# Weights loaded by piece into six tiles, later output stores, and the inverse's exchange issued by GpSimd

## The chip, the cores and the metric

The kernel runs on one core of one Trainium2 chip. The metric is the device time of one execution in microseconds, lower is better. The core has five engines that run their own instruction streams in order: TensorE (PE; weight loads are shown as PEld), VectorE (DVE), ScalarE (ACT), GpSimd (POOL) and SyncE (SP), which here only issues transfers. Transfers (DMA) run beside all of them.

## The reference

One layer of a hybrid decoder: 256 tokens, width 2048, all in float32. A gated delta rule branch (16 query and key heads, 32 value heads of 128) and an mLSTM branch (8 heads) run side by side on the same normalised input; their outputs are projected, gated, merged, projected again and added to the input.

```python
shift, scale, gate = jnp.split(jax.nn.silu(c) @ w_ada + b_ada, 3, axis=-1)
h = rms_norm(x, norm_pre_w) * (1.0 + scale[:, None]) + shift[:, None]
proj = h @ w_in
...
o_a = gated_delta_rule(q_a, k_a, v_a, g_log, beta)      # chunks of 64, a unit lower triangular solve in each
o_a = rms_norm(o_a, gdn_norm_w) * jax.nn.silu(gdn_z)
y_a = o_a @ w_proj_gdn
...
h_b = mlstm_chunkwise(q_b, k_b, v_b, ml_i + mlstm_b_i, ml_f + mlstm_b_f)
h_b = jax.nn.sigmoid(ml_o) * rms_norm(h_b, mlstm_norm_w) * jax.nn.silu(ml_z)
y_b = h_b @ w_proj_mlstm
merged = jax.nn.sigmoid(gate_a) * y_a + jax.nn.sigmoid(gate_b) * y_b
out = merged @ w_out
return x + gate[:, None] * rms_norm(out, norm_post_w)
```

The matrices hold some 375 MB, and each is read once. Products keep float32 accuracy with two parts of each operand: a high part `hi` in the narrower type float32r and the rest `lo`, so that one product is `hi*hi + hi*lo + lo*hi`, three passes of TensorE (`mm3`, L245 to L247).

## The kernel before

**The weight stream.** `Stream` (L64) holds a list of weight units in the order of the program. A unit is one load of up to 128 x 2048 float32 (1 MB) into one of three tiles `raw` (`load_w`, L161). It is used in pieces of 1024 columns: `prep_w` (L205) has ACT cast a piece into `whi` (L176) and DVE subtract to give `wlo` (L180), four buffers of each, and then `use` runs the products of the piece on TensorE (L247 for token-major results `pn`, `py`, `pw`; L658 and L662 for transposed ones `pt`). `_loads` issues the load of a unit as soon as the unit three places before it has had its last piece split, so a slot comes free after both of its halves have been split.

**Side work.** Beside the products of each piece, generators in `Side` emit the instructions of the recurrences; a `yield` puts the rest one piece (a step) later, `wait(n)` n steps. The order on every engine is thus fixed when the program is built. All transfers but a handful are issued by SP, in program order, and one that waits holds up those behind it.

**One period of the delta rule branch** (`gdn_period`, eight of them, `zg` 0 to 7; some 80 us each) loads the weights of two pairs of heads (`z` 0 and 1), and emits for each pair `gdn_stage1`: rows `gb` are fetched (L740), GpSimd masks them (`dd`, L747), ACT takes exponentials (L755 to L757), and DVE forms the matrices `au` (L816). `block_rows` (L894) then stores the 32 x 32 diagonal blocks to `ud` in DRAM (L900, four transfers for each pair). `base_inverse` (L903) inverts them: fetch `ug` from `ud` (L909, four transfers, each block broadcast four times), 32 rows of substitution on DVE over `xx` (L928 to L934), store `xx` to `xd` (L937, one transfer), and fetch it turned as `xcmp` (L941, four transfers). These 4 + 4 + 4 + 1 + 4 = 17 transfers are the exchange. From `xcmp`, ACT and DVE fill `x0`, `ycmp` and `y0` (L945 to L950), and `gdn_stage2` (L957) doubles the blocks on TensorE: `mp` (L978), its copy `pcm` (ACT, L983), `mx` (L994), `mq` and `mz` (L1012, with the copy `p` of L1018 between), then `pa` (L1039, which needs the values `rr` that ACT scales at L889), `pb`, `pc` and `po`. The normalised result goes through `oT` (L1110) to `o_dr` in DRAM (L1112); the output projections read it later (`ya`). The substitution and the stage 2 of one period run in the next one or two periods.

Four mLSTM groups follow, with the gate units between (a 1 MB unit of `w_ada` that DVE alone multiplies and adds, L1306 to L1313), then the output projections `py`, the merge and `pw`.

Of the kernel before, what the change touches and what calls it, by code (L numbers as in the profile page):

```python
# [7 lines left out]
F32 = mybir.dt.float32  # L8
F32R = mybir.dt.float32r
AF = mybir.ActivationFunctionType  # L10
ALU = mybir.AluOpType
# [4 lines left out]
P = 128  # L16
S = 256
D = 2048
KC = D // P
# [12 lines left out]
class Side:  # L32
# [4 lines left out]
    def __init__(self):  # L37
        self.gens = []
        self.t = 0
        self.debt = 0.0  # L40
# [23 lines left out]
class Stream:  # L64


    def __init__(self, load, side, ahead=3):
        self.side, self.ahead = side, ahead
        self.load = (load, "w", 3)
        self.units, self.items, self.rings = [], [], {}  # L70
        self.loaded = self.used = self.prepared = self.pending = 0

    def add(self, src, prep, use, pieces=2, after=None, on_load=None, load=None):
        load, ring, bufs = load or self.load
        r = self.rings.setdefault(ring, [])
        u = dict(src=src, prep=prep, use=use, after=after, on_load=on_load, load=load, done=False,
                 before=r[-bufs] if len(r) >= bufs else None)
        r.append(u)
        i = len(self.units)
        self.units.append(u)  # L80
        for h in range(pieces):
            self.items.append((i, h, h == pieces - 1))

    def _loads(self):

        while self.loaded < len(self.units):
            u = self.units[self.loaded]
            if u["before"] is not None and not u["before"]["done"]:
                return
            u["raw"] = u["load"](u["src"])  # L90
            if u["on_load"]:
                u["on_load"]()
            self.loaded += 1

    def run(self):
        self._loads()
        while self.used < len(self.items):
            while self.prepared < len(self.items) and self.pending <= self.ahead:
                i, h, last = self.items[self.prepared]
                u = self.units[i]  # L100
                self.pending += u["use"] is not None
                u["p", h] = u["prep"](h, u["raw"])
                u["done"] = last
                self.prepared += 1
                self._loads()
            i, h, last = self.items[self.used]
            u = self.units[i]
            self.used += 1
            if u["use"]:
                self.pending -= 1  # L110
                u["use"](h, *u["p", h])
            if last and u["after"]:
                u["after"]()
            if u["use"]:
                self.side.step()
# [3 lines left out]
def hybrid_layer_kernel(  # L119
# [25 lines left out]
    V, A, T, G, SP = nc.vector, nc.scalar, nc.tensor, nc.gpsimd, nc.sync  # L145
# [3 lines left out]
    wp = ctx.enter_context(tc.tile_pool(name="wp", bufs=2))  # L149
# [8 lines left out]
        SP.dma_start(t, src)  # L158
        return t

    def load_w(src):  # L161
        raw = wp.tile([P, 2048], F32, name="raw", tag="raw", bufs=3)
        c = 0
        for i, s_ in enumerate(src if isinstance(src, tuple) else (src,)):
            if isinstance(src, tuple) and len(s_.shape) == 3:
                SP.dma_start(raw.rearrange("p (k g c) -> p k g c", k=4, g=2)[:, :, i], s_)
                continue
            dst = raw[:, c:c + s_.shape[1] * (s_.shape[2] if len(s_.shape) == 3 else 1)]
            c += dst.shape[1]
            if len(s_.shape) == 3:  # L170
                dst = dst.rearrange("p (k n) -> p k n", k=s_.shape[1])
            SP.dma_start(dst, s_)
        return raw

    def split(src, hi, lo, eng=None):
# [10 lines left out]
    def split_w(src, hi, lo):  # L186

        n = src.shape[1]
        if early:
            eng = early.pop(0)  # L190
            A.copy(hi, src)
            for c in (slice(0, 512), slice(512, 1024)) if eng is G else (slice(0, 1024),):
                low(src[:, c], hi[:, c], lo[:, c], eng)
            if len(early) == 5:
                for k in (10, 12):
                    x_scale(k)
            return
        share[0] += share[1] * n
        if share[0] >= n:
            share[0] -= n  # L200
            split(src, hi, lo, G)
        else:
            split(src, hi, lo)

    def prep_w(h, raw, width=2048):  # L205
        n = min(1024, width - h * 1024)
        hi = wp.tile([P, 1024], F32R, name="whi", tag="whi", bufs=4)
        lo = wp.tile([P, 1024], F32R, name="wlo", tag="wlo", bufs=4)
        if begin:
            begin.pop()(raw[:, 0:n], hi, lo)  # L210
            return hi, lo
        split_w(raw[:, h * 1024:h * 1024 + n], hi[:, 0:n], lo[:, 0:n])
        return hi, lo

    freed = [-1] * 4
# [10 lines left out]
    def gfree(t):  # L226
        freed[slots[1].pop(id(t))[0]] = side.t
# [21 lines left out]
    side = Side()  # L249
    bp = x0 = y0 = None  # L250
# [3 lines left out]
    sil = cp.tile([P, KC], F32, name="sil")  # L254
# [42 lines left out]
    def ada_tile():  # L297
        return sp.tile([P, 2048], F32, name="ar", tag="ar", bufs=ADA_BUFS)

    def load_ada(src):  # L300
        raw = ada_tile()
        SP.dma_start(raw, src)
        return raw
# [114 lines left out]
    stream = Stream(load_w, side, 1)  # L418
# [315 lines left out]
    def wait(n):  # L734
        for _ in range(n):
            yield
# [157 lines left out]
    def block_rows(res, z):  # L894

        if z == 0:
            res["ud"] = dr.tile([4, 8, 32, 32], F32, name="ud", tag="ud", bufs=2)
        auv = res["au", z].rearrange("p h (b c) -> p (h b) c", b=2)
        for q in range(4):
            SP.dma_start(res["ud"][q, 4 * z:4 * z + 4].rearrange("m j i -> j m i"),  # L900
                         auv[32 * q:32 * q + 32, :, 256 + 32 * q:288 + 32 * q])

    def base_inverse(zg, res, zr):  # L903

        ud = res["ud"]
        xd = dr.tile([8, 4, 4, 8, 32], F32, name="xd", tag="xd", bufs=2)
        ug = bp.tile([P, 32, 32], F32, name="ug", tag="ug", bufs=1)
        for q in range(4):
            SP.dma_start(ug[32 * q:32 * q + 32],  # L909
                         ud[q].rearrange("m j i -> m (j i)").unsqueeze(0).broadcast_to([4, 8, 1024]))  # L910
        yield from wait(5)
        most = ROOM_US if zg else FIRST_ROOM_US
# [6 lines left out]
        xx = bp.tile([P, 8, 32], F32, name="xx", tag="xx", bufs=1)  # L919
        tmp = bp.tile([P, 8, 2, 32], F32, name="tmp", tag="tmp", bufs=1)  # L920
        V.tensor_copy(xx, eunit)
        for i in range(1, 32, 2):
            w = min(2, 32 - i)
            nq = (i + w - 2) // 4 + 1
            n = i + w
# [8 lines left out]
                V.scalar_tensor_tensor(xx[:, 0:nq, i + 1], xx[:, 0:nq, i], nsu[:, i // 2:i // 2 + 1],  # L934
                                       xx[:, 0:nq, i + 1], op0=ALU.mult, op1=ALU.add)
        yield from wait(1)
        SP.dma_start(xd.rearrange("qq q rg m i -> (q rg m) qq i"), xx)  # L937
        yield from wait(2)
        xcmp = bp.tile([P, 8, 32], F32, name="xcmp", tag="xcmp", bufs=1)
        for q in range(4):  # L940
            SP.dma_start(xcmp[32 * q:32 * q + 32], xd[:, q])  # L941
        yield from wait(3)
        side.debt += 1.1
        ycmp = bp.tile([P, 8, 32], F32, name="ycmp", tag="ycmp", bufs=1)
# [1 line left out]
        for q in range(4):  # L946
            c = slice(32 * q, 32 * q + 32)
# [9 lines left out]
    def gdn_stage2(zg, res, zr):  # L957
# [15 lines left out]
        for j in range(4):  # L973
            for i in range(2):
                m = 2 * j + i
                for t in range(2):
                    r, o = 64 * t, 64 * t + 32
                    T.matmul(pss[t][(o, r)[i]:(o, r)[i] + 32, j * 32:(j + 1) * 32], um(m)[r:r + 32, o:o + 32],  # L978
                             yc[r:r + 32, m], start=True, stop=True)
        for t in range(2):  # L980
            r, o = 64 * t, 64 * t + 32
# [7 lines left out]
        for j in range(4):  # L989
            for i in (1, 0):  # L990
                m = 2 * j + i
# [40 lines left out]
        rr = res["rr"].rearrange("p b z (h d) -> p b (z h d)", h=2)  # L1032
# [39 lines left out]
        for z in range(2):  # L1072
            junk = bp.tile([P, P], F32, name="junk", tag="sq", bufs=1)
            for blk in range(2):
                for h in range(2):
# [9 lines left out]
                               op0=ALU.mult, op1=ALU.add)  # L1085
# [18 lines left out]
        for z in range(2):  # L1104
            for h in range(2):
                for blk in range(2):
                    T.transpose(pts[z][:, h * S + blk * P:h * S + (blk + 1) * P], ons[z][:, blk, h], ident)
        for z in range(2):
            oT = bp.tile([P, 2, S], F32, name="oT", tag="oT")
            A.activation(oT.rearrange("p h t -> p (h t)"), pts[z], AF.Copy, scale=late_c["gnw"][:, 0:1])  # L1110
            gfree(pts[z])
            SP.dma_start(o_dr[4 * zg + 2 * z:4 * zg + 2 * z + 2].rearrange("h d t -> d h t"), oT)  # L1112

    def period_tail(zg, ps, qs, res, zr):
# [180 lines left out]
    gate_half = []  # L1295

    def add_gate_unit():

        gate_at[1] += KC
        if gate_at[1] < 34 or gate_at[0] == KC:  # L1300
            return
        gate_at[1] -= 34
        i = gate_at[0]
        gate_at[0] += 1

        def prep(h, raw):  # L1306
            side.debt += 2.4
            for q in range(2):
                if i == 0:
                    gate_half.append(bp.tile([P, 1024], F32, name=f"gacc{q}", tag=("ug", "rr")[q], bufs=1 + q))  # L1310
                    V.tensor_scalar(gate_half[q], raw[:, q * 1024:(q + 1) * 1024], sil[:, 0:1], None, op0=ALU.mult)
                else:
                    V.scalar_tensor_tensor(gate_half[q], raw[:, q * 1024:(q + 1) * 1024], sil[:, i:i + 1],  # L1313
                                           gate_half[q], op0=ALU.mult, op1=ALU.add)
            if i == KC - 1:
                side.add(gate_sum())
            return ()
        stream.add(w_ada[32 + i], prep, None, 1)

    def gate_sum():  # L1320
        yield
# [312 lines left out]
```

## Time and profile before

| | us |
|---|---|
| median of 3 runs (lowest to highest) | 1574.93 (1571.59 to 1575.77) |
| profiled execution, its time | 1578.37 |
| profiled execution, span from first to last instruction | 1576.6 |
| mean granted TensorE clock | 0.995 of full |
| busy: ACT, POOL | 971.1, 269.9 |
| DMA: 397.49 MB, mean | 252 GB/s |

The page's busy time counts an engine as busy from the start of an instruction to its end; a matmul's end is modelled. POOL is busy nearly only in the first 240 us. From 400 to 1000 us the eight periods show in the slices of the page: one slice of 39.4 us with DVE at 95% busy, the next with it at 80% and DMA at 85%. In the rows, "start, length, engine, line, operation, out<-in" stand in that order, and a bracket tells how long the engine stood idle before and what ended that.

### The profile page before, as it was taken

To read this page: it belongs to the slowest core of one execution; us is meant where nothing else is said; L and a number is where in the kernel's file an instruction comes from. 1 tells how busy PE (TensorE), PEld (TensorE's weight loads), DVE (VectorE), ACT (ScalarE), POOL (GpSimd) and SP (SyncE) were. 2 spreads that over 40 slices of the span, in tenths; PEclk is the share of its full clock that TensorE was granted. 3 is DMA by queue.
4 is the path that set the end of the run, shared out by engine and by line. 5 is a ranking of instruction groups with operands and counts; after the bars stand their busy time and mean duration, and the time that the engine had idled before them with its cause. 6 is when DMAs were issued, how large, how long until landed. Compare 5 with 4: busy or idle time off the path is not lost.

```text
span 1576.6 us, 22531 instructions
## 1 busy us (share of the span) xinstructions
PE 1554.4 (99%) x8256; PEld 1297.2 (82%) x8256; DVE 1172.0 (74%) x1781; ACT 971.1 (62%) x1638; POOL 269.9 (17%) x213
## 2 busy tenths in 40 slices
PE   8999999999999999999999999999999999999998
PEld 5888888888888888888888888888888888888886
DVE  6786556867798988898979797866768766756654
ACT  7754446767566767676768676666566554544443
POOL 6787761001010101010101010100000000100100
PEclk9999999999999999999999999999999999999999
DMA  9998785975767685868586857656879877766573
GB/s 377 404 386 325 270 294 185 295 242 197 247 221 238 197 263 183 256 193 257 180 246 197 235 194 234 212 200 233 295 260 332 321 270 297 283 238 236 216 270 107
DMA packets 185956, 397.49 MB, mean 252 GB/s; under 512 B 27595, under 2 KB 137825, under 8 KB 158325
## 3 DMA queue, kind: packets, MB, share of 16 engines
q1 hardware_dynamic: 185460, 395.44, 73.2%
q8 instruction: 65, 1.06, 0.3%
q10 hardware_dynamic: 290, 0.53, 0.1%
q14 instruction: 45, 0.37, 0.1%
q0 software_dynamic: 96, 0.09, 0.0%
HBM read 375.37 MB, written 20.64 MB: 251 GB/s over the span
## 4 chain that ended last, share of the span: by engine, by line
PE 61%; issue 14%; DMA 12%; ACT 6%; DVE 5%; POOL 1%; SPq 1%; DVEq 0%; ACTq 0%; POOLq 0%
PE pn L247 37%; PE py L247 8%; PE pt L658 7%; DMA raw<-in_dram 7%; PE pt L662 3%; DMA xcmp<-xd 2%; DVE wlo L180 2%; ACT whi L176 2%; POOL mg L1424 1%; DMA ud<-au 1%; DMA ar<-in_dram 1%; DVE au L816 1%; PE pa L1039 1%; SPq L909 1%; DMA xd<-xx 0%
## 5 line engine op out<-in xcount | busy, mean ns | idle before, releaser
L247 PE MATMUL pn<-whi,h 128*128 128x512 f32 x2304 | 729.1, 392 | 1.0 <-ACT part L493 0.5
L180 DVE TENSOR_TENSOR wlo<-raw,whi 128x1024 fp32r<-128x1024 f32 (+1 forms) x455 | 558.3, 1235 | 210.9 <-ACT whi L176 207.3
L176 ACT CAST whi<-raw 128x1024 fp32r<-128x1024 f32 x508 | 524.1, 1045 | 281.3 <-PE pn L247 155.3
L247 PEld LDWEIGHTS pn<-whi,h 128*128 128x128 f32 x2304 | 432.6, 188 | 91.1 <-ACT h L176 1.1
L247 PE MATMUL pn<-wlo,h 128*128 128x512 f32 x1152 | 448.6, 389 | 0.2 <-POOL wlo L180 0.2
L247 PEld LDWEIGHTS pn<-wlo,h 128*128 128x128 f32 x1152 | 216.5, 188 | 43.4 <-POOL wlo L180 0.8
L658 PE MATMUL pt<-h,whi 128*128 128x512 f32 x768 | 249.6, 407 | 0.0
L247 PE MATMUL py<-whi,y 128*128 128x512 f32 x768 | 239.9, 391 | 0.0
L662 PEld LDWEIGHTS pt<-h,wlo 128*128 128x128 f32 x768 | 146.8, 191 | 34.9
L247 PEld LDWEIGHTS py<-whi,y 128*128 128x128 f32 x768 | 144.2, 188 | 30.3 <-issue 0.6
L180 POOL TENSOR_TENSOR wlo<-raw,whi 128x1024 fp32r<-128x1024 f32 (+1 forms) x67 | 146.5, 2197 | 45.0 <-ACT whi L176 41.3
L662 PE MATMUL pt<-h,wlo 128*128 128x256 f32 x768 | 153.3, 281 | 0.0
L247 PE MATMUL py<-wlo,y 128*128 128x512 f32 x384 | 149.5, 389 | 0.0
L658 PEld LDWEIGHTS pt<-h,whi 128*128 128x128 f32 x768 | 120.3, 192 | 2.4
L747 POOL TENSOR_SCALAR_AFFINE_SELECT dd<-gb 128x256 f32<-128x256 f32 x40 | 36.7, 941 | 451.8 <-DMA gb<-rows 322.6
L176 ACT CAST y<-ya 128x512 fp32r<-128x512 f32 x48 | 29.9, 622 | 129.5 <-PE py L247 119.0
L491 DVE TENSOR_TENSOR part<-pn,part 128x512 f32<-128x512 f32 x112 | 73.7, 685 | 44.9 <-PE pn L247 44.7
L180 DVE TENSOR_TENSOR y<-ya,y 128x512 fp32r<-128x512 f32 x48 | 33.2, 691 | 75.4 <-ACT y L176 75.3
L247 PEld LDWEIGHTS py<-wlo,y 128*128 128x128 f32 x384 | 72.1, 188 | 14.9
L247 PE MATMUL pw<-whi,m 128*128 128x512 f32 x256 | 80.0, 391 | 0.0
L437 DVE SCALAR_TENSOR_TENSOR ar<-ar,csil 128x2048 f32<-128x2048 f32 x30 | 68.3, 2278 | 6.1 <-DMA ar<-in_dram 6.1
L928 DVE TENSOR_TENSOR tmp<-xx,ug 128x6 f32<-128x6 f32 (+15 forms) x128 | 65.4, 511 | 3.2
(272 smaller groups left out, 1475.0 us busy)
## 6 DMA issues: line engine op xcount, KB each, us to landing
raw<-in_dram SPq DMA_DIRECT2D x227, 1024.0 KB
raw<-in_dram SPq DMA_DIRECT2D x80, 512.0 KB
ar<-in_dram SPq DMA_DIRECT2D x31, 1024.0 KB
v<-vd SPq DMA_DIRECT2D x24, 512.0 KB
cw<-conv_dr SPq DMA_DIRECT2D x32, 256.0 KB
ya<-o_dr SPq DMA_DIRECT2D x32, 256.0 KB
gate_dr<-part SPq DMA_DIRECT2D x11, 512.0 KB
gb<-rows SPq DMA_DIRECT2D x20, 256.0 KB
```

The source lines that it names most:

```text
L176: A.copy(hi, src)
L180: eng.tensor_tensor(lo, src, hi.bitcast(F32), op=ALU.subtract)
L247: T.matmul(ps, l, r, start=start and i == 0, stop=stop and i == 2, skip_group_check=True)
L437: V.scalar_tensor_tensor(raw, raw, 1.0, csil, op0=ALU.mult, op1=ALU.mult, accum_out=ad[:, pt * KC + k:pt * KC + k + 1])
L491: V.tensor_tensor(part[g][:, b], ps[b], part[g][:, b], op=ALU.add)
L658: T.matmul(ps, hi[:, o:o + P], h2[:, k].rearrange("p a s -> p (a s)"), start=k == 0, stop=k == KC - 1, skip_group_check=True)
L662: T.matmul(ps[:, 0:S], lo[:, o:o + P], h_hi[:, k], start=False, stop=k == KC - 1, skip_group_check=True)
L747: G.affine_select(dd[:, :, blk * S:blk * S + P], gb[:, :, blk * P:(blk + 1) * P], pattern=[[0, 2], [1, P]], compare_op=ALU.is_ge, fill=-1e ...
L816: V.scalar_tensor_tensor(au[:, h, c0:c0 + 2 * n].rearrange("p (a b) -> p a b", a=2), ps_[:, 0:2 * n].rearrange("p (a b) -> p a b", a=2), c ...
L909: SP.dma_start(ug[32 * q:32 * q + 32], ud[q].rearrange("m j i -> m (j i)").unsqueeze(0).broadcast_to([4, 8, 1024]))
L928: V.tensor_tensor(tmp[:, 0:nq, 0:w, 0:n], xx[:, 0:nq, 0:n].unsqueeze(2).broadcast_to([P, nq, w, n]), ug[:, 0:n, i:i + w].rearrange("p k c ...
L1039: T.matmul(pa[:, c], x0[:, 2 * g], rr[:, 0, c], start=True, stop=True)
```

## The change

Five edits, one in the stream, four around it:

1. The stream's item is a piece rather than a unit. `raw` is 128 x 1024 (512 KB) with six tiles rather than 128 x 2048 with three, so the room is the same. A slot comes free when its own piece has been split; `load_w` loads one half of a unit. Where a unit came from two sources side by side, each piece takes two transfers of half the size.
2. The 17 transfers of the exchange (`ud`, `ug`, `xd`, `xcmp`) are issued by GpSimd (`G.dma_start`) rather than by SP.
3. The two stores of `oT` to `o_dr` in a period come two and four steps later, except in the last period.
4. A gate unit becomes two pieces, with the same two DVE instructions.
5. The split reads `raw[:, 0:n]`, since the piece is the tile.

TensorE, DVE and ACT run the same instructions in the same order as before.

```diff
 class Stream:
-        self.load = (load, "w", 3)
-        self.units, self.items, self.rings = [], [], {}
+        self.load = (load, "w", 6)
+        self.items, self.rings = [], {}
     def add(self, src, prep, use, pieces=2, after=None, on_load=None, load=None):
-        u = dict(src=src, prep=prep, use=use, after=after, on_load=on_load, load=load, done=False,
-                 before=r[-bufs] if len(r) >= bufs else None)
-        r.append(u)
-        i = len(self.units)
-        self.units.append(u)
         for h in range(pieces):
-            self.items.append((i, h, h == pieces - 1))
+            u = dict(src=src, h=h, prep=prep, use=use, after=after if h == pieces - 1 else None,
+                     on_load=on_load if h == 0 else None, load=load, done=False,
+                     before=r[-bufs] if len(r) >= bufs else None)
+            r.append(u)
+            self.items.append(u)
     def run(self):
...
-                u["done"] = last
+                u["done"] = True
...
-    def load_w(src):
-        raw = wp.tile([P, 2048], F32, name="raw", tag="raw", bufs=3)
...
+    def load_w(src, h):
+        raw = wp.tile([P, 1024], F32, name="raw", tag="raw", bufs=6)
+        if not isinstance(src, tuple):
+            if len(src.shape) == 3:
+                k = 1024 // src.shape[2]
+                SP.dma_start(raw.rearrange("p (k n) -> p k n", k=k), src[:, h * k:(h + 1) * k])
+            else:
+                SP.dma_start(raw, src[:, h * 1024:(h + 1) * 1024])
+            return raw
+        if len(src[0].shape) == 3:
+            for i, s_ in enumerate(src):
+                SP.dma_start(raw.rearrange("p (k g c) -> p k g c", k=2, g=2)[:, :, i], s_[:, 2 * h:2 * h + 2])
+            return raw
...
-        split_w(raw[:, h * 1024:h * 1024 + n], hi[:, 0:n], lo[:, 0:n])
+        split_w(raw[:, 0:n], hi[:, 0:n], lo[:, 0:n])
...
         for q in range(4):
-            SP.dma_start(res["ud"][q, 4 * z:4 * z + 4].rearrange("m j i -> j m i"),
+            G.dma_start(res["ud"][q, 4 * z:4 * z + 4].rearrange("m j i -> j m i"),
                          auv[32 * q:32 * q + 32, :, 256 + 32 * q:288 + 32 * q])
...
         for q in range(4):
-            SP.dma_start(ug[32 * q:32 * q + 32],
+            G.dma_start(ug[32 * q:32 * q + 32],
                          ud[q].rearrange("m j i -> m (j i)").unsqueeze(0).broadcast_to([4, 8, 1024]))
...
-        SP.dma_start(xd.rearrange("qq q rg m i -> (q rg m) qq i"), xx)
+        G.dma_start(xd.rearrange("qq q rg m i -> (q rg m) qq i"), xx)
...
         for q in range(4):
-            SP.dma_start(xcmp[32 * q:32 * q + 32], xd[:, q])
+            G.dma_start(xcmp[32 * q:32 * q + 32], xd[:, q])
...
+        oTs = []
         for z in range(2):
             oT = bp.tile([P, 2, S], F32, name="oT", tag="oT")
             A.activation(oT.rearrange("p h t -> p (h t)"), pts[z], AF.Copy, scale=late_c["gnw"][:, 0:1])
             gfree(pts[z])
+            oTs.append(oT)
+        for z, oT in enumerate(oTs):
+            if zg < 7:
+                yield from wait(2)
             SP.dma_start(o_dr[4 * zg + 2 * z:4 * zg + 2 * z + 2].rearrange("h d t -> d h t"), oT)
```

On GpSimd, in the period `zg` = 4 (around 668 to 710 us before), the program before has the selects and small operations of the two pairs alone (`b` and `sk` are small vectors that ACT needs, `so` those of the output's norm):

```order
L747 AFFINE_SELECT dd<-gb 128x2x128 x2
L780 TENSOR_TENSOR b_6209<-gb,ngt 128x2
L243 TENSOR_TENSOR so<-so,mhalf 128x8
L243 TENSOR_TENSOR sk<-sse,phalf 128x2
L747 AFFINE_SELECT dd<-gb 128x2x128 x2
L780 TENSOR_TENSOR b_6408<-gb,ngt 128x2
L243 TENSOR_TENSOR sk<-sse,phalf 128x2
```

The same place on GpSimd after the change:

```order
L753 AFFINE_SELECT dd<-gb 128x2x128 x2
L786 TENSOR_TENSOR b_6451<-gb,ngt 128x2
L249 TENSOR_TENSOR so<-so,mhalf 128x8
L249 TENSOR_TENSOR sk<-sse,phalf 128x2
L906 DMA ud<-au 32x4x32 x4
L753 AFFINE_SELECT dd<-gb 128x2x128 x2
L786 TENSOR_TENSOR b_6654<-gb,ngt 128x2
L943 DMA xd<-xx 128x8x32
L249 TENSOR_TENSOR sk<-sse,phalf 128x2
L906 DMA ud<-au 32x4x32 x4
L947 DMA xcmp<-xd 32x1x256 x4
L915 DMA ug<-ud 32x1x1024 x4
```

The first pair's four `ud` now stand ahead of the second pair's two selects, and after the second pair's `ud` come `xcmp` of the period before and `ug` of this one.

On SP, in the second half of the same period, the program before has (`v` and `cw` are shifted values and taps of a convolution, `vd` its buffer in DRAM; each `raw` row is one load of 1 MB):

```order
L900 DMA ud<-au 32x4x32 x4
L172 DMA raw<-in_dram 128x8x256
L937 DMA xd<-xx 128x8x32
L172 DMA raw<-in_dram 128x8x256
L843 DMA v_6525<-vd 128x2x512
L849 DMA cw<-conv_dr 128x2x256 x2
L900 DMA ud<-au 32x4x32 x4
L941 DMA xcmp<-xd 32x1x256 x4
L172 DMA raw<-in_dram 128x8x256
L1112 DMA o_dr<-oT 128x2x256 x2
L909 DMA ug<-ud 32x1x1024 x4
L172 DMA raw<-in_dram 128x8x256
```

The same place on SP after the change (a `raw` row of 128x4x256 is 512 KB, of 128x2x256 half of that, for the next units, which come from two sources):

```order
L164 DMA raw<-in_dram 128x4x256 x4
L849 DMA v_6775<-vd 128x2x512
L164 DMA raw<-in_dram 128x4x256
L855 DMA cw<-conv_dr 128x2x256 x2
L164 DMA raw<-in_dram 128x4x256 x3
L1123 DMA o_dr<-oT 128x2x256
L170 DMA raw<-in_dram 128x2x256 x4
L1123 DMA o_dr<-oT 128x2x256
```

The four 1 MB loads stand as eight loads of 512 KB with nothing of the exchange between them, and the stores to `o_dr` come behind the last of them rather than ahead.

More of the change, by code (lines that the diff above doesn't have):

```diff
@@ L75, in add @@
         r = self.rings.setdefault(ring, [])
-        u = dict(src=src, prep=prep, use=use, after=after, on_load=on_load, load=load, done=False,
-                 before=r[-bufs] if len(r) >= bufs else None)
-        r.append(u)
-        i = len(self.units)
-        self.units.append(u)
-        for h in range(pieces):
-            self.items.append((i, h, h == pieces - 1))
+        for h in range(pieces):
+            u = dict(src=src, h=h, prep=prep, use=use, after=after if h == pieces - 1 else None,
[3 more added lines that the diff above has]
+            self.items.append(u)
     def _loads(self):
-        while self.loaded < len(self.units):
-            u = self.units[self.loaded]
+        while self.loaded < len(self.items):
+            u = self.items[self.loaded]
             if u["before"] is not None and not u["before"]["done"]:
                 return
-            u["raw"] = u["load"](u["src"])
+            u["raw"] = u["load"](u["src"], u["h"])
             if u["on_load"]:
@@ L98, in run @@
             while self.prepared < len(self.items) and self.pending <= self.ahead:
-                i, h, last = self.items[self.prepared]
-                u = self.units[i]
+                u = self.items[self.prepared]
                 self.pending += u["use"] is not None
-                u["p", h] = u["prep"](h, u["raw"])
-                u["done"] = last
+                u["p"] = u["prep"](u["h"], u["raw"])
+                u["done"] = True
                 self.prepared += 1
                 self._loads()
-            i, h, last = self.items[self.used]
-            u = self.units[i]
+            u = self.items[self.used]
             self.used += 1
@@ L110, in run @@
                 self.pending -= 1
-                u["use"](h, *u["p", h])
-            if last and u["after"]:
+                u["use"](u["h"], *u["p"])
+            if u["after"]:
                 u["after"]()
@@ L159, in const @@
         return t
-    def load_w(src):
-        raw = wp.tile([P, 2048], F32, name="raw", tag="raw", bufs=3)
[L163 to L172, printed above, removed]
+    def load_w(src, h):
[11 more added lines that the diff above has]
+            return raw
+        c = -h * 1024
+        for s_ in src:
+            n = s_.shape[1]
+            a, b = max(0, -c), min(n, 1024 - c)
+            if a < b:
+                SP.dma_start(raw[:, c + a:c + b], s_[:, a:b])
+            c += n
         return raw
@@ L298, in ada_tile, with load_ada @@
         return sp.tile([P, 2048], F32, name="ar", tag="ar", bufs=ADA_BUFS)
-    def load_ada(src):
+    def load_ada(src, h=0):
         raw = ada_tile()
@@ L1306, in prep @@
         def prep(h, raw):
[L1307 to L1315, printed above, removed]
+            side.debt += 1.2
+            if i == 0:
+                gate_half.append(bp.tile([P, 1024], F32, name=f"gacc{h}", tag=("ug", "rr")[h], bufs=1 + h))
+                V.tensor_scalar(gate_half[h], raw, sil[:, 0:1], None, op0=ALU.mult)
+            else:
+                V.scalar_tensor_tensor(gate_half[h], raw, sil[:, i:i + 1], gate_half[h], op0=ALU.mult, op1=ALU.add)
+            if i == KC - 1 and h == 1:
                 side.add(gate_sum())
             return ()
-        stream.add(w_ada[32 + i], prep, None, 1)
+        stream.add(w_ada[32 + i], prep, None)
     def gate_sum():
```

## The prediction

> **What bounds the kernel now.** I read the page's sums first, then the TensorE waits, the granted clock, the chain of waits, and SP's rows in the stretch that the chain names.
>
> ```profile
> span 1576.6 us, 22531 instructions
> PE 1554.4 (99%) x8256; PEld 1297.2 (82%) x8256; DVE 1172.0 (74%) x1781; ACT 971.1 (62%) x1638; POOL 269.9 (17%) x213
> ```
>
> TensorE is busy all but 22 us, and the change leaves its instructions and their order alone. So no transfer that becomes cheaper is worth anything by itself. Only three things count: time in which TensorE stands still, time in which its clock is reduced, and new waits.
>
> The TensorE waits from 400 to 1100 us (waiting instruction, what released it, total, times, longest), and the sums of five stretches (length, busy time of PE, PEld, DVE, ACT and POOL, granted clock, DMA share, GB/s):
>
> ```profile
> PE pa L1039 <- ACT rr L889: 5.4, 4, 1.9
> PE mx L994 <- ACT pcm L983: 2.2, 3, 1.2
> PE mz L1012 <- ACT p L1018: 1.5, 1, 1.5
> 480.00:500.00 20.00, 18.80 (x202) 15.95 (x201) 13.43 (x38) 14.88 (x33) 0.00 (x0) 1.00 0.79 243
> 720.00:740.00 20.00, 18.12 (x110) 15.54 (x109) 14.70 (x41) 11.72 (x20) 0.00 (x0) 0.91 0.73 229
> 800.00:820.00 20.00, 18.18 (x109) 15.62 (x109) 15.01 (x41) 11.13 (x21) 0.00 (x0) 0.91 0.77 229
> 880.00:900.00 20.00, 18.47 (x122) 15.62 (x121) 14.95 (x39) 10.81 (x19) 0.00 (x0) 0.91 0.81 236
> 950.00:990.00 40.00, 37.92 (x300) 32.44 (x299) 30.32 (x63) 23.62 (x42) 0.00 (x0) 0.96 0.72 233
> ```
>
> The waits are 5.4 + 2.2 + 1.5 = 9.1 us. Four of these stretches also lost clock: 3 x 20 x 0.09 + 40 x 0.04 = 7.0 us, some 1.75 us for each wait of about 1.5 us or more. The 1.2 us wait near 490 cost no clock (1.00 there). **The ceiling is 9.1 + 7.0 = 16.1 us, 1.0%.** The rest of the idle time lies at the start and end, where nothing that sets the order changes.
>
> The Trainium skill, "TensorE: Matmul & The Clock Gate", section "HAM oscillation — how this bites in real kernels", wants no idle gap above about 3.4 us. By that rule these waits would cost no clock and the ceiling would be 9.1 us; the 0.91 in the rows disagrees, and I go by the rows.
>
> Who makes the waits? The chain in the period around 700 us (start, length, what), then the rows of SP, ACT and DVE there:
>
> ```profile
> 697.15 5.20 DMA raw<-in_dram
> 702.37 4.02 DMA xcmp<-xd
> 710.67 14.02 DMA raw<-in_dram
> 728.94 0.53 ACT rr L889
> 729.51 2.01 PE pa L1039 x8
> ...
> 692.66 0.38 SPq L937 DMA_DIRECT2D xd<-xx  x1
> ...
> 700.39 1.86 SPq L900 DMA_DIRECT2D ud<-au  x4
> 702.37 3.81 SPq L941 DMA_DIRECT2D xcmp<-xd  x4
> 706.27 0.40 SPq L172 DMA_DIRECT2D raw<-in_dram  x1
> 706.77 1.03 SPq L1112 DMA_DIRECT2D o_dr<-oT  x2
> 707.86 2.71 SPq L909 DMA_DIRECT2D ug<-ud  x4
> ...
> 700.28 2.55 DVE L180 TENSOR_TENSOR wlo<-raw,whi 128x1024 fp32r<-128x1024 f32 x2
> 703.88 1.22 DVE L180 TENSOR_TENSOR wlo<-raw,whi 128x1024 fp32r<-128x1024 f32 x1
> 722.17 0.09 DVE L915 MEMSET ug<- 128x32 f32 x1 [2.05 <-DMA ug<-ud]
> 724.76 1.05 ACT L176 CAST whi<-raw 128x1024 fp32r<-128x1024 f32 x1 [5.71 <-DMA raw<-in_dram]
> ```
>
> ACT runs in order and stood 5.71 us for a weight load; the value scaling (`rr`, L889) queued behind that cast came late, and so did `pa`. That load was issued at 710.67, though the split that freed its slot ended at 705.10 (counting splits in pairs back from it). SP had been in `ud`, `xcmp`, a load, `o_dr` and `ug`. It then took 14.02 us against 5.20 for an equal load at 697.15, because it lay behind `ug` in one queue: `ug` was issued by 710.57, and DVE got it only at 722.17. These are two faults, and the change addresses both.
>
> **The change part by part.** *Pieces and queue.* With six slots of 1024 columns the first half of that load is freed by the split that ends at 702.83, 2.3 us before the second, and SP is no longer held by `ud`, `xcmp` and `ug`. So it goes 5 to 8 us earlier, half as long, without 12 us of `ug` ahead of it in SP's queue, and with `o_dr` two steps back. ACT needed it only about 2 us earlier: `pa` waited 1.88 of ACT's 5.71 us. I count all four `pa` waits, the `mz` wait (in the stretch 950 to 990, also behind a late cast) and the clock as gone: 5.4 + 1.5 + 7.0 = 13.9 us. If half of them stayed it would be 7. SP issues some 25% more transfers (860 for 692); 168 x 0.40 us = 67 us.
>
> ```profile
> SPq L172 <- DVE wlo L180: 590.4, 157, 7.0
> ACT x L948 <- DMA xcmp<-xd: 21.9, 7, 5.7
> ```
>
> SP's waits for DVE's splits alone are 590.4 us over the whole run, so the issue time is hidden; if it were not, loads would be late again and the cost is bounded by the 13.9 us above.
>
> *The exchange on GpSimd.* It has 17 transfers a period. What the trace shows of GpSimd as issuer is three transfers at the start. Here are the last two, and the last one's median time from issue to landing:
>
> ```profile
> 2.07 0.56 POOL L313 DMA_DIRECT2D npre<-in_dram  x1
> 2.61 0.54 POOL L313 DMA_DIRECT2D con<-in_dram  x1
> con<-in_dram POOLq DMA_DIRECT2D x1, 64.0 KB, 6.4
> ```
>
> An issue occupies GpSimd for e = 0.55 us. Landing after the end of issue, L, has an upper end of 6.4 - 0.55 = 5.8 us, with DMA saturated. The lower end is SP's own: the last `xcmp` was issued by 706.18 and DVE had it at 707.74, 1.5 us. I take 2.7: `xcmp` itself is the nearer row, but freed loads now run beside it.
>
> ```profile
> 685.79 2.74 POOL L747 TENSOR_SCALAR_AFFINE_SELECT dd<-gb 128x256 f32<-128x256 f32 x2 [2.90 <-DVE au L816]
> 688.53 0.40 ACT L755 ACTIVATE dd<-dd,ngt 128x128 f32<-128x128 f32 x1
> 690.95 1.99 ACT L176 CAST whi<-raw 128x1024 fp32r<-128x1024 f32 x2
> 692.55 1.22 DVE L180 TENSOR_TENSOR wlo<-raw,whi 128x1024 fp32r<-128x1024 f32 x1
> 696.21 1.06 ACT L176 CAST whi<-raw 128x1024 fp32r<-128x1024 f32 x1 [1.66 <-PE pn L247]
> 699.50 0.86 DVE L816 SCALAR_TENSOR_TENSOR au<-psb,cj,dd 128x256 f32<-128x256 f32 x2
> 706.41 1.73 ACT L948 COPY x<-xcmp 32x256 f32<-32x256 f32 x4 [2.81 <-DMA xcmp<-xd]
> 707.74 0.45 DVE L945 STREAM_TRANSPOSE ycmp<-xcmp 128x256 f32<-128x256 f32 x1 [0.97 <-DMA xcmp<-xd]
> 712.57 1.06 ACT L983 COPY pcm<-mp 32x128 f32<-32x128 f32 x4
> 714.02 0.21 PE L994 MATMUL mx<-xcmp,pcm 32*32 32x32 f32 x1
> ```
>
> In GpSimd's order the first pair's four `ud` now stand ahead of the second pair's two selects. ACT's exponentials start the moment the selects end (688.53), so they slip 4e = 2.2 us, the casts behind them too, and the split of 692.55 by about 1.5 (first cast done at 694.1). DVE's rows show no idle time from there until `au` ends at 700.36, so the second pair's `au` slips by 4e - 0.7 = 1.5 us. TensorE does not feel that: casts are a full ring ahead of it (the cast at 696.21 waited 1.66 us for TensorE). Then come four `ud` and four `xcmp` on GpSimd: 8e = 4.4 us, and L. Before, `xcmp` was complete 7.3 us after `au`. So it arrives later by (4e - 0.7) + 8e + L - 7.3 = **12e + L - 8.0 = 1.3 us**. ACT's `pcm` ended at 713.63 and TensorE wanted it at 714.02: 0.4 us of cover. A wait of 0.9 us at `mx` is left, without loss of clock, in about five periods (the middle ones, built alike): 4.5 us. The present 2.2 us are inside the ceiling. `xd` (1024 runs against 128 in the rows above: 0.55 us, or 4.4 if the time goes by runs) goes at 692.66 and has 10 us until `xcmp`; `ug` waits for `ud` as before and leads its use at 722 by several us.
>
> The Trainium skill, "SBUF — State Buffer", section "SBUF: two separate sides", speaks against such a move: descriptors of a GpSimd transfer starve while DVE runs a two-port operation such as an f32 copy. By that rule e would grow by the length of such copies. DVE's rows between 699.50 and 705.10 are two-input operations, which that page excepts; no row here shows the starving.
>
> *Later stores, split gate units:* the same work, later in SP's order, and `o_dr` is read only in the output projections, after the mLSTM part. Nothing, either way.
>
> **Sum.** Profiled execution: 1576.6 - 16.1 + 4.5 = 1565.0 us of span. The profiled execution took 1578.4 us and the median of the runs is 1574.9, so I carry the difference, -11.6 us, to the median: **1563 us**.
>
> **Rivals.** (1) *The exchange is not late at all:* e = 0.46 (SP's own issue of `ud`, 1.86/4) and L = 1.5 give -1.0 us; no wait at `mx`, 1574.9 - 16.1 = 1559. For it: the `xcmp` transfers no longer queue behind SP's loads; against: only the start shows GpSimd as issuer.
>
> (2) *The exchange becomes the bound:* the same sum with e = 0.55 and L = 5.8 gives 4.4 us, thus 4.0 us at `mx`, and every such wait also costs 1.75 us of clock: 5 x 5.75 = 29 us against 16: 1588. From 12e + L - 8.0 = 2.8 us on (e = 0.68, or L = 4.2) it is slower by more than 0.3%, since 5 x (2.4 + 1.75) = 20.8. For it: ACT waits for `xcmp` seven times already (21.9 us), and `mx` has 0.4 us of cover; against: at the start the queue held 8 KB rows at saturation.
>
> (3) *In between:* 2.0 to 2.8 us late, clock lost at each wait: 5 x 3.4 to 5 x 4.2 us against 16, so 1575 to 1579.
>
> (4) *The move does nothing for the loads:* `ug` hinders the load as before, since both go through the same DMA engines, and the `pa` waits stay, about 1575. The Trainium skill, "DMA: Bandwidth & Descriptors", section "Issuing engines are not separate DMA queues", says so in general: another issuer saves only issue time. Against: an equal load took 5.20 us, and what differed for the one of 14.02 us was the `ug` ahead of it in the same queue.
>
> **Chances.** Forecast 0.50, (1) 0.13, (2) 0.20, (3) 0.10, (4) 0.07. A measurement of this kernel can tell about 0.3% (4.7 us) from no change. Faster: 0.50 + 0.13 = 0.63; same: (3) and (4), 0.17; slower: 0.20. The range runs from (1), 1557 with some scatter, to 1585, which leaves out the upper part of (2).
>
> **What would show it.** Right: no `pa` wait and a PEclk of 1.00 between 700 and 990; ACT's casts no longer wait for `raw`; POOL rows for `ud` of about 0.55 us; `mx` waits of 0.5 to 1.3 us in the middle periods. Wrong: ACT waiting longer than 4 us for `xcmp`, a clock of 0.91 at the `mx` waits, `ud` rows of 0.7 us or more on POOL (rival 2), or a cast waiting for `raw` next to `pa` (rival 4).

## The result and the profile after

The changed kernel takes 1590.25 us, the median of 6 runs (1588.52 to 1595.47); the kernel before took 1574.24 us beside it. The ratio is 1.0105, with a 95% interval of 1.0087 to 1.0123: **slower by 16 us**. I had forecast 1563 us with 1585 as the upper end. Two runs of one experiment below (the kernel before with only `ug` on GpSimd) took 2212 and 2594 us at a granted clock of 0.66 and 0.56 for the whole run, and are left out.

The page of the changed kernel first, its span and busy times:

```profile
span 1588.3 us, 23422 instructions
PE 1556.2 (98%) x8256; PEld 1299.9 (82%) x8256; DVE 1175.1 (74%) x1781; ACT 972.9 (61%) x1638; POOL 343.1 (22%) x349
```

TensorE stands still for 1588.3 - 1556.2 = 32.1 us, where before it was 22.2. The waits of the changed kernel from 400 to 1100 us (waiting instruction, what released it, total, times, longest):

```profile
ACT x L954 <- DMA xcmp<-xd: 46.5, 8, 9.5
DVE ycmp L951 <- DMA xcmp<-xd: 19.1, 7, 3.7
PE mp L984 <- DVE ycmp L951: 10.6, 5, 3.6
PE mx L1000 <- ACT pcm L989: 7.0, 5, 2.1
```

The `pa` and `mz` waits are gone, as forecast. But TensorE now waits twice in a period for the inverse: 17.6 us in place of 9.1. The clock falls at these places (stretches of 14 us; the columns are those of the sums by stretch in the prediction):

```profile
552.00:566.00 14.00, 11.87 (x144) 9.99 (x143) 10.89 (x20) 10.59 (x19) 0.00 (x0) 0.88 0.71 198
634.00:648.00 14.00, 10.75 (x137) 9.15 (x138) 10.60 (x19) 11.07 (x21) 0.16 (x1) 0.88 0.78 227
716.00:730.00 14.00, 11.09 (x139) 9.24 (x138) 9.01 (x12) 11.21 (x22) 1.14 (x2) 0.88 0.76 228
798.00:812.00 14.00, 10.32 (x118) 8.59 (x117) 7.22 (x11) 10.05 (x19) 1.71 (x3) 0.76 0.65 201
882.00:896.00 14.00, 10.93 (x139) 9.06 (x138) 8.47 (x11) 10.68 (x21) 1.14 (x2) 0.88 0.75 219
964.00:978.00 14.00, 11.47 (x130) 9.58 (x129) 9.01 (x12) 11.10 (x20) 1.94 (x4) 0.88 0.81 236
```

That is 5 x 14 x 0.12 + 14 x 0.24 = 11.8 us of clock, where I read 7.0 before. Waits and clock together: 29.4 against 16.1 us, 13.3 more; the spans differ by 1588.3 - 1576.6 = 11.7.

The chain of waits in the period around 700 us (start, length, what):

```profile
706.38 0.80 DVE au L822 x2
...
709.70 7.50 DMA xcmp<-xd
...
718.94 1.05 ACT whi L182
720.00 1.28 ACT L1137
...
724.46 0.70 PE mx L1000 x38
```

And the rows of GpSimd, SP, ACT, DVE and TensorE there (start, length, engine, line; in brackets the idle time before and what ended it):

```profile
699.11 0.94 POOL L943 DMA_DIRECT2D xd<-xx  x1 [3.00 <-DVE xx L938]
...
707.47 2.25 POOL L906 DMA_DIRECT2D ud<-au  x4 [4.33 <-DVE au L822]
709.70 2.19 POOL L947 DMA_DIRECT2D xcmp<-xd  x4
...
708.33 3.77 SPq L164 DMA_DIRECT2D raw<-in_dram  x3
...
717.23 1.68 ACT L954 COPY x<-xcmp 32x256 f32<-32x256 f32 x4 [7.80 <-DMA xcmp<-xd]
723.34 1.06 ACT L989 COPY pcm<-mp 32x128 f32<-32x128 f32 x4
...
717.90 0.45 DVE L951 STREAM_TRANSPOSE ycmp<-xcmp 128x256 f32<-128x256 f32 x1 [2.62 <-DMA xcmp<-xd]
...
718.50 0.45 PE L984 MATMUL mp<-ycmp,au 32*32 32x32 f32 x32 [1.94 <-DVE ycmp L951]
724.46 0.24 PE L1000 MATMUL mx<-xcmp,pcm 32*32 32x32 f32 x2 [0.96 <-ACT pcm L989]
```

An issue on GpSimd takes 2.25 / 4 = 0.56 us, as I had it. The landing doesn't: the last `xcmp` was issued by 709.70 + 2.19 = 711.89 and DVE had it at 717.90, **L = 6.0 us** where I had put 2.7. Meanwhile SP, no longer busy with the exchange, issued three more weight loads from 708.33 on. ACT stood 7.80 us for `xcmp`, and the casts and the table load that were due in that time came between it and `pcm`: so `mx` waited again after `mp`.

### The profile page after: what moved, and what is told of

Read it like the earlier page. It is cut to its first block, busy times and chain, and to the rows that moved or that the text cites. A ratio compares the mean times of both kernels' runs of the same rounds, so it can differ in the third digit from the quotient of the medians.

```text
span 1588.3 us, 23422 instructions
## 1 busy us (share of the span) xinstructions
PE 1556.2 (98%) x8256; PEld 1299.9 (82%) x8256; DVE 1175.1 (74%) x1781; ACT 972.9 (61%) x1638; POOL 343.1 (22%) x349
## 4 chain that ended last, share of the span: by engine, by line
PE 76%; issue 13%; DMA 4%; DVE 3%; ACT 2%; POOL 1%; SPq 0%; DVEq 0%; ACTq 0%; POOLq 0%
PE pn L253 45%; PE pt L664 10%; PE py L253 8%; PE pt L668 5%; DVE wlo L186 1%; DMA xcmp<-xd 1%; DMA raw<-in_dram 1%; DMA o_dr<-oT 1%; ACT whi L182 1%; PE psa L253 1%; DVE au L822 1%; DMA gs<-gate_dr 0%; PE csil L325 0%; PE pb L1053 0%; PE pc L1063 0%
## 5 line engine op out<-in xcount | busy, mean ns | idle before, releaser
L753 POOL TENSOR_SCALAR_AFFINE_SELECT dd<-gb 128x256 f32<-128x256 f32 x40 | 23.1, 599 | 313.2 <-DMA gb<-rows 278.8
```

The costliest lines, as they stand in the source:

```text
L753: G.affine_select(dd[:, :, blk * S:blk * S + P], gb[:, :, blk * P:(blk + 1) * P], pattern=[[0, 2], [1, P]], compare_op=ALU.is_ge, fill=-1e ...
```

## The experiments

**Theory A:** the exchange lands late on GpSimd's queue, and this is the whole loss. **Theory B:** the pieces cause it, since more loads in flight collide with the exchange whoever issues it. Later A is split in two. A1: the loads that SP now starts during the exchange take the DMA engines. A2: the order on GpSimd, with `xcmp` behind the second pair's `ud`.

### Only the pieces, only the queue

All 17 transfers back to SP, in the changed kernel:

```diff
-            G.dma_start(res["ud"][q, 4 * z:4 * z + 4].rearrange("m j i -> j m i"),
+            SP.dma_start(res["ud"][q, 4 * z:4 * z + 4].rearrange("m j i -> j m i"),
...
-            G.dma_start(ug[32 * q:32 * q + 32],
+            SP.dma_start(ug[32 * q:32 * q + 32],
...
-        G.dma_start(xd.rearrange("qq q rg m i -> (q rg m) qq i"), xx)
+        SP.dma_start(xd.rearrange("qq q rg m i -> (q rg m) qq i"), xx)
...
-            G.dma_start(xcmp[32 * q:32 * q + 32], xd[:, q])
+            SP.dma_start(xcmp[32 * q:32 * q + 32], xd[:, q])
```

> The changed kernel with all 17 transfers of the exchange issued by SP again; pieces and later stores stay. Theory A (the loss comes from the exchange landing late on GpSimd's queue): the waits of ACT and DVE for xcmp fall from 46.5 and 19.1 us to near the 21.9 of before, the mp and mx waits of TensorE fall under 4 us, and the time is 1562 to 1574 us; some pa waits of before can stay, since ug is in SP's queue again. Theory B (the loss comes from the pieces: more loads in flight collide with the exchange whoever issues it): xcmp waits stay over 40 us and the time stays at 1584 us or more.

Measured: 1560.59 us, ratio 0.9909 (0.9892 to 0.9925). Its page and its waits from 400 to 1100 us:

```profile
span 1559.4 us, 23408 instructions
PE 1545.2 (99%) x8256; PEld 1291.4 (83%) x8256; DVE 1172.3 (75%) x1781; ACT 972.5 (62%) x1638; POOL 267.6 (17%) x213
...
ACT x L954 <- DMA xcmp<-xd: 20.7, 8, 4.1
ACT whi L182 <- DMA raw<-in_dram: 1.7, 1, 1.7
PE mx L1000 <- ACT pcm L989: 0.9, 3, 0.5
```

No `pa` wait, 14.2 us of idle time, and 11.0 us less PE time than in the changed kernel for the same matmuls: the stretches of reduced clock are gone too (mean granted clock 0.999, against 0.991). Theory B falls.

The other half alone, in the kernel before: the same four places from `SP.dma_start` to `G.dma_start`, and nothing else.

> The kernel before with nothing but the 17 transfers of the exchange issued by GpSimd (three tiles of 2048 columns, stores as before). Theory A: the landings of xcmp are late here too, mp and mx waits of 10 us or more in all, 1580 to 1592 us. Theory B: without pieces the DMA has room, xcmp lands within 3 us of its issue, no mp wait, 1560 to 1570 us.

Measured: 1590.51 us, ratio 1.0098 (1.0082 to 1.0113). Waits from 400 to 1100 us:

```profile
ACT x L948 <- DMA xcmp<-xd: 40.3, 10, 8.5
PE mx L994 <- ACT pcm L983: 11.0, 6, 2.4
PE mp L978 <- DVE ycmp L945: 7.6, 5, 3.1
```

The queue alone makes the whole loss, 15.7 us against the 1574.79 of the kernel before that was measured beside it, and with it the pieces change nothing: 1590.5 without, 1590.25 with them. The `pa` waits are gone here too, so either part removes them, and the second one finds nothing left to gain.

### Which of the transfers

In the changed kernel, only `ug` on GpSimd:

```diff
-            G.dma_start(res["ud"][q, 4 * z:4 * z + 4].rearrange("m j i -> j m i"),
+            SP.dma_start(res["ud"][q, 4 * z:4 * z + 4].rearrange("m j i -> j m i"),
...
-        G.dma_start(xd.rearrange("qq q rg m i -> (q rg m) qq i"), xx)
+        SP.dma_start(xd.rearrange("qq q rg m i -> (q rg m) qq i"), xx)
...
-            G.dma_start(xcmp[32 * q:32 * q + 32], xd[:, q])
+            SP.dma_start(xcmp[32 * q:32 * q + 32], xd[:, q])
```

> The changed kernel with only the four ug of each period issued by GpSimd; ud, xd and xcmp are on SP. Theory A: xcmp is as early as before (ACT's wait for it about 22 us or less), ug no longer stands ahead of weight loads, so the pa waits are gone and the mx waits stay small: 1558 to 1567 us, the fastest of the four. Theory B: 1584 us or more. A third theory, that ug hinders loads whoever issues it: pa waits as before, about 1575 us.

Measured: 1560.96 us, ratio 0.9912 (0.9898 to 0.9927), the same as with all on SP and not the fastest of the four as I had said. It leaves 13.8 us of idle time in place of 14.2: with pieces the place of `ug` in SP's queue costs nothing.

Only `xcmp` back on SP; `ud`, `xd` and `ug` stay on GpSimd:

```diff
-            G.dma_start(xcmp[32 * q:32 * q + 32], xd[:, q])
+            SP.dma_start(xcmp[32 * q:32 * q + 32], xd[:, q])
```

> The changed kernel with only the four xcmp issued by SP; ud, xd and ug stay on GpSimd. Theory A, if the landing of ud on GpSimd's queue matters as much as that of xcmp: xcmp waits for ud no more, only for xd and the tile, so it is issued when SP reaches it, and lands 2 to 4 us later; ACT's wait for xcmp falls to 25 us or less and the time to 1565 to 1573 us. If SP's own queue of loads ahead of xcmp takes as long as GpSimd's path does: xcmp lands 5 us or more after its issue, and the time is 1580 us or more.

Measured: 1565.51 us, ratio 0.9941 (0.9926 to 0.9956). ACT waits 23.1 us for `xcmp`, TensorE 3.8 us at `mx`, never at `mp`. Moving four of the 17 transfers back recovers most of the loss. Here `xcmp` no longer stands behind the `ud` that wait for `au`; SP reached it 0.5 us after the first of those was issued, and it landed some 4 us after the end of its issue, on SP too. So a late landing isn't a property of GpSimd's queue alone.

### Order or company

Only `ud` back on SP:

```diff
-            G.dma_start(res["ud"][q, 4 * z:4 * z + 4].rearrange("m j i -> j m i"),
+            SP.dma_start(res["ud"][q, 4 * z:4 * z + 4].rearrange("m j i -> j m i"),
```

> The changed kernel with only the eight ud of each period issued by SP; xd, xcmp and ug stay on GpSimd. Theory A2 (GpSimd's queue is in order, and the second pair's ud, which takes 7.3 us to land, stands ahead of xcmp): xcmp lands within 3 us of the end of its issue instead of 5.9, ACT's wait for it is under 25 us in all, 1560 to 1566 us. Theory A1 (SP no longer stands still while the exchange runs, and its weight loads take the DMA engines): ud lands in some 4 us as on SP before, but xcmp still shares the engines and lands 4 to 6 us after its issue; 1570 to 1582 us.

Measured: 1562.40 us, ratio 0.9929 (0.9905 to 0.9953). The time is A2's, but not for the reason I gave: `xcmp` took 4.8 us to land in the median (from 600 to 960 us), from the start of its issue, where A2 had it within 3 us. It was issued far earlier, as GpSimd's rows show:

```profile
689.84 0.98 POOL L943 DMA_DIRECT2D xd<-xx  x1 [4.24 <-DVE xx L938]
...
693.65 2.22 POOL L947 DMA_DIRECT2D xcmp<-xd  x4 [0.40 <-issue]
705.31 2.38 POOL L915 DMA_DIRECT2D ug<-ud  x4 [9.45 <-DMA ud<-au]
```

With no `ud` ahead of it, it went 3.8 us after `xd`; in the changed kernel it went 10.6 us after (699.11 and 709.70). The next kernel keeps all 17 transfers on GpSimd and only turns that order round:

```diff
-        yield from wait(2)
+        yield from wait(1)
         xcmp = bp.tile([P, 8, 32], F32, name="xcmp", tag="xcmp", bufs=1)
...
-        yield from wait(3)
+        yield from wait(4)
         side.debt += 1.1
```

> The changed kernel with xcmp issued one step earlier, so that in GpSimd's order it stands ahead of the second pair's four ud (and no longer waits for au with them); all 17 transfers stay on GpSimd. If the place of xcmp behind ud in GpSimd's order is what makes it late: it is issued near 702 us instead of 709.7 in the period around 700 us, ACT's waits for xcmp fall under 20 us, no mp wait, 1559 to 1566 us. If GpSimd as issuer costs in another way (late selects, the second pair's au): 1580 us or more.

Measured: 1560.73 us, ratio 0.9919 (0.9890 to 0.9948). GpSimd's rows, and ACT's wait from 400 to 1100 us, where `mp` and `mx` have none:

```profile
693.95 2.25 POOL L947 DMA_DIRECT2D xcmp<-xd  x4
698.32 2.21 POOL L906 DMA_DIRECT2D ud<-au  x4 [2.11 <-DVE au L822]
...
ACT x L954 <- DMA xcmp<-xd: 3.2, 2, 2.4
```

One step in the order takes back all of the loss. GpSimd as issuer, its 17 issues, the late second pair (its `au` 15.7 us behind the first pair's, as in the changed kernel, against 14.8 before): all still there, and free. The earlier place is also a quieter one: from 693.95 to 698.20 the DMA share was 0.64, and `xcmp` landed in 3.8 us in the median (600 to 960 us), though SP was as free to load as in the changed kernel.

Is the landing itself a matter of A1? This kernel leaves the changed order alone and holds SP while the exchange runs:

```diff
                          auv[32 * q:32 * q + 32, :, 256 + 32 * q:288 + 32 * q])
+        if z == 1:
+            SP.dma_start(dr.tile([1, 8], F32, name="hold", tag="hold", bufs=2), res["au", 1][0:1, 0, 0:8])
...
             G.dma_start(xcmp[32 * q:32 * q + 32], xd[:, q])
+        SP.dma_start(dr.tile([4, 8], F32, name="held", tag="held", bufs=2), xcmp[0:P:32, 0, 0:8])
```

> The changed kernel with two tiny transfers a period added to SP's order: one of 32 bytes that waits for the second pair's au, and one that waits for xcmp to have landed. SP then stands still between them, as it did when it issued the exchange itself, and starts no weight load. Theory A1: ud and xcmp have the DMA engines to themselves after what was already queued; xcmp lands 2 to 4 us after the end of its issue, TensorE's mp wait is gone, 1562 to 1572 us. Theory A2: xcmp lands 5 to 6 us after its issue as now, and the time stays at 1582 us or more.

Measured: 1569.55 us, ratio 0.9974 (0.9961 to 0.9988). GpSimd's and DVE's rows of this kernel, then its waits:

```profile
701.39 2.24 POOL L906 DMA_DIRECT2D ud<-au  x4 [4.33 <-DVE au L822]
703.63 2.17 POOL L949 DMA_DIRECT2D xcmp<-xd  x4
...
708.29 0.45 DVE L954 STREAM_TRANSPOSE ycmp<-xcmp 128x256 f32<-128x256 f32 x1
...
ACT x L957 <- DMA xcmp<-xd: 24.5, 8, 4.8
PE mx L1003 <- ACT pcm L992: 5.2, 5, 1.6
```

The last `xcmp` was issued by 703.63 + 2.17 = 705.80 and used at 708.29: L is at most 2.5 us in place of 6.0, with the same issuer and the same order. It is so in the other periods too. The median time from the start of an issue to its landing, from 600 to 960 us, in the changed kernel and then with SP held (count, size, us):

```profile
xcmp<-xd POOLq DMA_DIRECT2D x19, 32.0 KB, 6.9
xcmp<-xd POOLq DMA_DIRECT2D x20, 32.0 KB, 3.3
```

The sums of the stretch from the issue of `xcmp` to its landing (columns as above; the last three are clock, DMA share, GB/s), in the changed kernel:

```profile
709.70:718.00 8.30, 6.86 (x34) 5.61 (x33) 3.33 (x4) 0.74 (x2) 4.44 (x9) 1.00 1.05 282
```

with SP held:

```profile
703.60:708.20 4.60, 4.60 (x23) 3.82 (x22) 3.26 (x3) 0.45 (x2) 3.71 (x8) 1.00 0.59 169
```

and with the whole exchange on SP (the kernel of the pieces alone):

```profile
700.10:705.00 4.90, 4.90 (x23) 4.04 (x23) 3.35 (x3) 1.14 (x3) 0.00 (x0) 1.00 0.58 149
```

The DMA engines are full in the first and little more than half busy in the other two. So L is A1's: the order is the same in the first two, and what differs is whether SP loads beside the exchange. SP's rows in the last of them show what the move to GpSimd took away:

```profile
698.24 1.84 SPq L906 DMA_DIRECT2D ud<-au  x4
700.12 3.32 SPq L947 DMA_DIRECT2D xcmp<-xd  x4
703.55 0.95 SPq L164 DMA_DIRECT2D raw<-in_dram  x2
```

While SP issued the exchange itself, for 5.2 us, it could start no load. The Trainium skill, "DMA: Bandwidth & Descriptors", section "Issuing engines are not separate DMA queues", says that transfers run on the same DMA engines and interleave whichever engine started them; the share of 1.05 with L = 6.0, against 0.59 with 2.5, agrees.

### What removes the pa waits

The kernel before, with only `ug` on GpSimd:

```diff
-            SP.dma_start(ug[32 * q:32 * q + 32],
+            G.dma_start(ug[32 * q:32 * q + 32],
```

> The kernel before with only the four ug of each period issued by GpSimd; tiles of 2048 columns. My prediction named two faults behind the late weight loads: the slot is freed in whole tiles, and ug stands ahead of the load in SP's queue. If ug is the one that decides: no pa wait, 1559 to 1566 us. If the whole tiles decide: the pa waits stay near 5 us and the time within 3 us of the kernel before. If either alone is enough: 1559 to 1566 us, and this agrees with the pieces alone (ug on SP) having 1560.6 us.

Three runs: 1559.55, 1560.48 and 1564.26 us, ratio 0.9923 (0.9894 to 0.9953). The same kernel once more, for its profile:

> The same kernel as the run before of this name (the kernel before with only the four ug on GpSimd), for a usable profile: no pa wait, ACT's waits for raw near 0, 1559 to 1565 us, if ug in SP's queue is what makes the weight load late. If pa waits are there all the same: about 1572.

Measured: 1561.29 us, ratio 0.9934 (0.9910 to 0.9957), with no `pa` wait. ACT's waits for weights, and SP's row for the load that the prediction followed:

```profile
ACT whi L176 <- DMA raw<-in_dram: 9.2, 7, 3.3
...
704.38 0.87 SPq L172 DMA_DIRECT2D raw<-in_dram  x1
```

ACT's waits were 31.1 us before (8 times, up to 6.9); they fell, but not near 0 as I had said. The whole period lies earlier here, so the load is counted from the first `xcmp` on SP (698.56 here, 702.37 before): it goes 5.8 us after it where it went 8.3 after it (710.67). These 2.5 us are about the 2.71 that the four `ug` took on SP. ACT cast the first half of that load at 715.90 without waiting for it, so it also landed within 11.5 us of the start of its issue, where it took 14.02. So whole tiles are no fault that needs mending if `ug` is off SP's queue; and the next run asks the reverse, with the pieces alone, all transfers on SP and the stores as before:

```diff
         for z, oT in enumerate(oTs):
-            if zg < 7:
-                yield from wait(2)
             SP.dma_start(o_dr[4 * zg + 2 * z:4 * zg + 2 * z + 2].rearrange("h d t -> d h t"), oT)
```

> The changed kernel with all 17 transfers on SP (1560.6 us) and the output stores issued together again, as in the kernel before; only the pieces stay. If the pieces alone remove the pa waits: within 3 us of 1560.6. If the two steps of the stores do: pa waits of some 5 us, 1570 to 1575 us.

Measured: 1561.27 us, ratio 0.9936 (0.9920 to 0.9953), no `pa` wait, 1.4 us at `mx`. The later stores do nothing that can be measured.

Last, all on SP, pieces, and `xcmp` one step earlier (the edit of the `wait` lines above):

> The changed kernel with all 17 transfers on SP and xcmp one step earlier, ahead of the second pair's ud. If what is left of ACT's wait for xcmp (20.7 us) and of the mx waits (0.9 us) comes from the same order: both near 0, 1559 to 1561 us, no more than 1 us faster than 1560.6, since TensorE stands still for less than that. If SP now stands before xd and its loads come late: casts wait for raw again, 1563 us or more.

Measured: 1560.01 us, ratio 0.9925 (0.9907 to 0.9943); ACT waits once for `xcmp`, 4.9 us, and `mx` 0.4 us. It is the lowest median of all, but within the scatter of the others between 1560.6 and 1561.3. With 13.7 us idle, the next gain isn't in these waits.

The idle time (span less PE busy) and the PE busy time of the profiled runs, side by side (the medians were not all measured together; the kernel before had medians of 1571.7 to 1574.8 beside them):

| kernel | median us | idle us | PE busy us |
|---|---|---|---|
| before | 1574.24 | 22.2 | 1554.4 |
| the change | 1590.25 | 32.1 | 1556.2 |
| queue only | 1590.51 | 33.6 | 1552.2 |
| SP held | 1569.55 | 20.6 | 1545.9 |
| `xcmp` on SP | 1565.51 | 17.2 | 1547.4 |
| `xcmp` first, all on GpSimd | 1560.73 | 14.1 | 1544.7 |
| pieces only | 1560.59 | 14.2 | 1545.2 |

## Why the prediction was wrong

**The ceiling was right.** Waits and clock of before were put at 16.1 us; pieces alone gain 14.2 us at the median and 17.2 us between the profiles (8.0 idle, 9.2 PE time). The forecast was this ceiling plus 4.5 us of waits at `mx`, so nearly all of the error lies in what the move of the queue costs.

**The two faults were one too many.** I named the whole tiles and `ug` ahead of the load, and said that the change addresses both. Each part alone removes all `pa` waits, so the gain was safe twice over, and the move of `ud`, `xd` and `xcmp` wasn't needed for it.

**The step that failed is L**, the landing of `xcmp` after its issue: put at 2.7 us, measured 6.0. I had bounded it by 1.5 and 5.8, and took the value near the lower row, because it was `xcmp` itself. But that row was measured while SP stood still for loads, since SP was issuing `ud` and `xcmp`. The move takes that away, and for "freed loads now run beside it" I added 1.2 us; the run with SP held shows that they cost 6.0 - 2.5 = 3.5. The upper row was the like one: the DMA share was 0.96 at the start (2 to 9 us, before) and 1.05 here.

The rest of the sum held. e was 0.56 us, and the one issue of `xd`, which I had bounded by 0.55 and 4.4, took 0.94. 12e + L - 8.0 with the measured L is 6.7 + 6.0 - 8.0 = 4.7 us late; by the rows `xcmp` is complete 717.90 - 707.18 = 10.7 us after the end of `au` against 707.74 - 700.36 = 7.4 (the prediction has 7.3), so 3.3 us later, and the second pair's `au` slipped another 0.9 against the first pair's (put at 1.5): 4.2. With SP held L is 2.5 and the sum gives 1.2 us, 0.8 of it at `mx`; four of the five waits there were 1.0 to 1.6 us.

**The wait came at another place as well.** I reckoned only with `mx`. The row of `mp` in the kernel before:

```profile
710.65 0.45 PE L978 MATMUL mp<-ycmp,au 32*32 32x32 f32 x32
```

`ycmp` ended there at 707.74 + 0.45 = 708.19, so `mp` had 2.5 us of cover, and 4.2 us of lateness went past it: 1.7 us by this count, 1.94 us in the period shown. The rest appears at `mx`, behind the casts that ACT had to catch up on. From 400 to 1100 us the two waits are 17.6 us, near the 20 that rival (2) gave with its 4.0 us in five places.

**The rivals.** (2), the exchange becomes the bound, is what happened: 1588 by its sum, 1590.25 measured, with its signs (ACT over 4 us for `xcmp`, reduced clock at the waits) and through L, above the 4.2 from which it decides. I gave it 0.20, and cut the range at 1585. (1) and (3) needed L of 4.2 us or less, and fell with 6.0. (4) fell: without pieces the move of the queue removed the `pa` waits. With `ug` alone on GpSimd the load went earlier by about what the four `ug` take at issue, and landed sooner as well.

**What neither sum nor rivals had** is the order. `xcmp` needs `xd`, which the changed kernel issued at 699.11, 10.6 us earlier; it stood behind `ud` that wait for `au`. I measured its lateness from `au`, as if that were its source. On SP this cost ACT 20.7 us of waiting and TensorE almost nothing; on GpSimd it costs 30 us of the kernel. With SP held the loss against pieces alone is 9.0 us (1569.55 against 1560.59; 10 if each is taken against the kernel before beside it), so some 20 of the 29.7 us hang on the loads that SP starts beside the exchange. But the causes don't add up as separate shares: one step in the order, with SP's loads left free, takes back all of it. What stays open is how the 9.0 us divide between GpSimd's issue times and the hold itself; TensorE waits 5.2 us at `mx` there, against 0.9 with pieces alone, and no cast of ACT waits for a load from 400 to 1100 us.

## What to carry to other kernels

An engine that issues transfers also holds back those behind them in its order. Whoever moves transfers to another queue should ask what the old issuer starts in the freed time, and take the latency from a stretch in which that runs, not from the quiet one that is going away. And before a queue is changed, look at what a late transfer waits for in its issuer's order: here one step earlier was worth the whole loss.

## What the runs showed of the hardware

- Small transfers of GpSimd were not served ahead of SP's loads: four of 32 KB took 7.5 us from the start of the first issue to ACT's use with DMA at a share of 1.05, and 4.1 us with SP held at a share of 0.59.
- The clock doesn't follow the length of a wait alone. With SP held, a wait of 1.36 us in the stretch from 625 to 655 went with a clock of 0.94, and one of 1.55 us from 786 to 816 with none lost:

```profile
625.00:655.00 30.00, 28.64 (x251) 24.48 (x251) 22.58 (x48) 21.06 (x38) 2.34 (x5) 0.94 0.78 241
...
786.00:816.00 30.00, 28.45 (x263) 24.57 (x262) 24.75 (x53) 22.66 (x41) 2.73 (x5) 1.00 0.81 261
```

My "1.75 us for each wait of about 1.5 us or more" is a mean, not a bound. Both waits are far below the 3.4 us that the Trainium skill gives in "TensorE: Matmul & The Clock Gate", section "HAM oscillation — how this bites in real kernels"; the 0.94 disagrees with it, the 1.00 doesn't.
